# Reordering a second attention stage: earlier head loads, softmax and rotated queries at a higher priority, and another pace for weight sums

## The chip, the cores and the metric

The kernel runs on one core of a Trainium2 chip. The metric is the device time of one execution in microseconds (us). A core has five engines that run side by side: TensorE (PE; its weight loads are shown as PEld), VectorE (DVE), ScalarE (ACT), GpSimd (POOL) and SyncE (SP). SP does no arithmetic here; it issues the DMA transfers between DRAM and the on-chip memory, in its own order. POOL issues a second kind of DMA, one that can add to what stands in DRAM.

## The reference

Two decoder layers over 1024 tokens of width 1024, in float32. Layer 0 is a chunkwise mLSTM mixer and an MLP. From its output a shared key/value latent is computed once. Layer 1 is latent attention over it, and an MLP. What matters here is the attention of layer 1 (8 heads, 128 plain and 64 rotated columns per head) and the MLPs:

```python
def block(args):                       # one block of 128 queries, all heads
    s = (einsum('bqhd,bkhd->bhqk', qn_b, k_nope)
         + einsum('bqhd,bkd->bhqk', qr_b, k_rope)) * scale
    s = where(kpos[None, :] <= qpos[:, None], s, -inf)
    p = softmax(s, axis=-1)
    return einsum('bhqk,bkhd->bqhd', p, v)

def sqrelu_mlp(h, w1, w2):             # 1024 -> 4096 -> 1024
    return square(relu(h @ w1)) @ w2
...
x = x + g1 * rmsnorm(mixer(modulate(rmsnorm(x))))
x = x + g2 * rmsnorm(sqrelu_mlp(modulate(rmsnorm(x)), w1, w2))
```

## The kernel before

**Number format.** Every dense operand is kept as a high and a low part in float32r, and a product is three matmuls (`mm3`, lines 255 to 257: low by high, high by low, high by high). A weight block of 128x1024 is loaded by SP into a `raw` buffer (line 236; four buffers), cast to the high part `wh` by ACT (L549 or L190) and subtracted to the low part `wl` by DVE (L550 or L191). Activations are split in the same way (`split_mod`, L531 on ACT and L532 on DVE).

**Two halves, two streams.** The 1024 tokens go through as two halves of 512. While one half runs its mixer, the other runs an MLP whose products keep TensorE full: `two_streams(dense, other)` takes steps from the two generators in turn, and `go` ties every step's TensorE work behind the last one's, so that TensorE's order is the order written in the code. Three such stretches follow one another: the MLP of layer 0 for the first half; the MLP of layer 0 for the second half beside `attention_first`; the MLP of layer 1 for the first half beside `attention_second`. After them the last MLP runs alone; it uses sums of weight blocks and needs fewer products for that.

**The order on the other engines.** The order of each engine's instructions is fixed when the program is built. A planner simulates the engines on estimated durations and takes, of the instructions that are ready, the one of the highest priority; without more, that is the one traced first. `prompt(f)` raises the priority of what `f` traces by 300 places (`PRIO`). The dense stream's weight loads, its hidden activations and its accumulations (`accumulate`, L199) have this; the splits of its weights have 40 (`CUT`). On the chip every engine then follows its list in order.

**Attention.** `prepare_pair` computes for a pair of heads the keys, values, plain queries and rotated queries (`rope`, then `query_rotary`: a cast on ACT, L1565, and four pieces on DVE, L1567 to L1570). In the second half keys and values are stored to DRAM (`kd`, L1646; `vd`, L1652), and so are the queries (`qd`, L1668) and the rotated queries (`td`, L1669). After the four pairs, `units` in `attention_second` goes over the heads one by one: `loaded_head` reads a head back (two `kd` loads at L1681, `qd` at L1683, `td` of the pair at L1686, two `vd` loads at L1689; 512 KB each), and its two groups of 256 queries follow. All these tiles share 24 buffers of the tag `k4`.

For a group, `scores` computes two score tiles (`score_mm`, L1584 to L1590, into the PSUM tile `pm`, of which there are two, shared with the dense stream) and runs `softmax` on each: maximum (L1594), scaling of it (L1595), both on DVE, exponential with row sum on ACT (L1596), reciprocal (L1597) and multiplication (L1598) on DVE, and for the first of the two a zeroing of 128 columns on POOL (L1600). The probabilities stand in `raw` buffers. `turned` transposes them on TensorE (L1704) and splits the result with `split_mod`; `products` multiplies by the values one dense step later.

**Weight sums.** `weight_sums` prepares in DRAM, with POOL's adding DMAs, the four sums of blocks of `mlp_w1[1]` that the last MLP needs: 16 chunks of eight transfers of 256 KB, each a step of the generator `wsums`. A step is a DVE flag (L1046), tied behind the dense stream's latest DVE instruction, a POOL copy that waits for it (L1047) and the DMA (L1050 if it adds, else L1052). The dense streams take a step each time they finish one of their own: `with_weight_sums` for the first two stretches, once 28 steps have been counted, and `with_rest` for the third, one each until the 128 are used up.

Of the kernel before, what the change touches and what calls it, by code (L numbers as in the profile page):

```python
# [83 lines left out]
def kernel(  # L84
# [408 lines left out]
    def last_of(g):  # L493

        while True:
            try:
                next(g)
            except StopIteration as e:
                return e.value
# [1062 lines left out]
    def query_rotary(qr):  # L1562
        T = k4v(F32R)
        hi = tmp(F32R)
        nc.scalar.copy(hi, qr)  # L1565

        nc.vector.tensor_copy(T[0:64, 0], hi[0:64].bitcast(F32))  # L1567
        nc.vector.tensor_copy(T[64:128, 1], hi[64:128].bitcast(F32))
        nc.vector.tensor_sub(T[64:128, 0], qr[0:64], hi[0:64].bitcast(F32))
        nc.vector.tensor_sub(T[0:64, 1], qr[64:128], hi[64:128].bitcast(F32))  # L1570
        return T

# [19 lines left out]
    def softmax(f, pr, n, even):  # L1592
        m, l = small(1), small(1)
        nc.vector.reduce_max(m, f, axis=AX.X, negate=True)  # L1594
        nc.vector.tensor_scalar(m, m, SCALE, None, ALU.mult)  # L1595
        nc.scalar.activation(pr[:, :n], f, AF.Exp, bias=m, scale=SCALE, accum_out=l)  # L1596
        nc.vector.reciprocal(l, l)  # L1597
        nc.vector.tensor_scalar(pr[:, :n], pr[:, :n], l, None, ALU.mult)  # L1598
        if even:
            nc.gpsimd.memset(pr[:, n : n + P], 0.0)  # L1600

    def scores(kk, unit):

        (_, q, kn, _), j = unit
        prs = []
        if j < 2:
            st = pm()
            pr = raw().rearrange("p (a b) -> p a b", b=512)
            for e in range(2):
                score_mm(lambda g: st[:, e], kk, q, kn, 2 * j + e)  # L1610
            for e in range(2):
                n = (2 * j + e + 1) * P
                softmax(st[:, e, :n], pr[:, e], n, e == 0)
                prs.append(pr[:, e])
        else:
            for e in range(2):
                st = pm()
                n = (2 * j + e + 1) * P
                score_mm(lambda g: st[:, g], kk, q, kn, 2 * j + e)
                pr = raw()  # L1620
                softmax(st.rearrange("p a b -> p (a b)")[:, :n], pr, n, e == 0)
                prs.append(pr)
        return prs

# [6 lines left out]
    def prepare_pair(p_, hf):  # L1631


        wr, wkv = w_pair_r(p_), w_pair_kv(p_)
        yield 0
        wn, pt = w_pair_n(p_), pc()
        for k in range(3):
            mm3(pt, wr[0][:, k], wr[1][:, k], hf.cq[0][k], hf.cq[1][k], k == 0, k == 2)
        rp = rope(pt, hf)
        next(rp)  # L1640
        kt = [k4v(F32R) for _ in range(2)]
        kn = [(t[:, 0], t[:, 1]) for t in kt]
        k_half(kn, wkv, hf)
        for r in range(2):
            for i in range(2):
                nc.sync.dma_start(kd[2 * p_ + r, i, :, ts(hf.i, H)], kn[r][i].bitcast(F32))  # L1646
        yield 1
        vt = [k4v(F32R, 256) for _ in range(2)]
        v = v_half(wkv, hf, vt)
        for r in range(2):  # L1650
            for i in range(2):
                nc.sync.dma_start(  # L1652
                    vd[2 * p_ + r, i, :, ts(hf.i, H)].rearrange("p (t e) -> p t e", e=P),
                    vt[i][:, :, ts(r, P)].bitcast(F32),
                )
        qn = []
        for r in range(2):
            t = k4v(F32R)
            pt = pc() if r else ps()
            for k in range(3):  # L1660
                s = ts(r, P)
                mm3(pt, wn[0][:, k, s], wn[1][:, k, s], hf.cq[0][k], hf.cq[1][k], k == 0, k == 2)
            split_mod(t[:, 0], t[:, 1], pt, None)
            qn.append(t)
        T = query_rotary(last_of(rp))
        if hf.i:
            for r in range(2):
                nc.sync.dma_start(qd[2 * p_ + r], flat(qn[r]))  # L1668
            nc.sync.dma_start(td[p_], flat(T))  # L1669
            yield 1  # L1670
        else:
            yield 2
        vs = [[(h_[:, ts(r, P)], l_[:, ts(r, P)]) for h_, l_ in v] for r in range(2)]
        return [(2 * p_ + r, (qn[r], T[:, r]), kn[r], vs[r]) for r in range(2)]
# [18 lines left out]
    def attend(hf, groups, dense, behind=lambda: None):  # L1693


        def turned(work):
            PTh, PTl = hdv(F32R, 256), hdv(F32R, 256)
            n = 0
            for u, b0, nb in work:
                for b in range(b0, b0 + nb, 2):  # L1700
                    pt = pc()
                    for e in range(2):
                        for i in range(2):
                            nc.tensor.transpose(  # L1704
                                pt[:, ts(2 * e + i, P)], u.prs[i][:, ts(b + e, P)], ident
                            )
                    s = slice(n, n + 2)
                    split_mod(PTh[:, s], PTl[:, s], pt.rearrange("p (a b) -> p a b", b=256), None)
                    n += 2
            return PTh, PTl  # L1710

        def products(work, PT):
            n = 0
            for u, b0, nb in work:
                if b0 == 0:
                    u.po = ps()[:, :256]
                for kb in range(b0, b0 + nb):
                    mm3(u.po, *u.v[kb], PT[0][:, n], PT[1][:, n], kb == 0, kb == u.nk - 1)
                    n += 1
                if b0 + nb == u.nk:  # L1720
                    s = ts(u.j % 2, 256)
                    if u.hh < 6:
                        o = tmp()[:, :256]
                        nc.scalar.copy(o, u.po)
                        nc.sync.dma_start(oT[ts(u.hh, P), ts(u.j, 256)], o)
                    else:
                        split_mod(hf.o.hi[u.hh][:, s], hf.o.lo[u.hh][:, s], u.po, None)

        def begin():
            us = []  # L1730
            for head, j in next(groups, []):
                u = Half()
                (u.hh, _, _, u.v), u.j, u.nk = head, j, 2 * j + 2
                u.prs = scores(hf.kk, (head, j))
                us.append(u)
            return us

        late = None
        yield "align"
        us = begin()  # L1740
        yield 1
        while us:
            if sum(u.nk for u in us) <= 4:
                rounds = [[(u, 0, u.nk) for u in us]]
            else:
                rounds = [[(u, b, min(4, u.nk - b))] for u in us for b in range(0, u.nk, 4)]
            for n, work in enumerate(rounds):
                if late:
                    late()
                PT = turned(work)  # L1750
                late = lambda a=(work, PT): products(*a)
                if len(rounds) == 1:
                    yield 1
                if n == len(rounds) - 1:
                    us = begin()
                    if not us:
                        behind()
                yield next(dense)
        late()
# [15 lines left out]
    def attention_second(hf):  # L1775
        pairs = [prepare_pair(p_, hf) for p_ in range(4)]
        next(pairs[0])
        yield 0
        for p_ in range(4):
            if p_ < 3:  # L1780
                yield from primed(pairs[p_], pairs[p_ + 1])
            else:
                yield from pairs[p_]

        def units():
            for hh in range(NH):
                h_ = loaded_head(hh)
                if hh == 6:
                    last_o(hf)
                for j in range(2, 4):  # L1790
                    yield [(h_, j)]

        yield from attend(hf, units(), cycle((1, 0.5, 0.5)), lambda: load_o(hf))
# [364 lines left out]
    wsums = weight_sums(mlp_w1[1])  # L2158
    steps_done = [0]

    def with_weight_sums(g):
        for v in g:
            if v != "within":
                steps_done[0] += 1
                if steps_done[0] > 28:
                    next(wsums, None)
            yield v

# [76 lines left out]
    def with_rest(g):  # L2245

        n = 0
        for v in g:
            if v != "within":
                n += 1  # L2250
                next(wsums, None)
                if n == 61:
                    later[0]()
            yield v
# [18 lines left out]
    n = 0  # L2273
# [34 lines left out]
```

## Time and profile before

| what | us |
|---|---|
| median of three runs | 2362.25 (2359.37 to 2362.75) |
| the profiled execution | 2359.22 |
| its span, first to last instruction | 2357.3 |
| TensorE busy | 2321.8 |
| VectorE busy | 1605.7 |
| ScalarE busy | 1098.2 |
| GpSimd busy | 155.0 |

The span is what the trace covers; the time is what the device reports and is 1.9 us longer. "Busy" is the time in which an engine has an instruction in work. TensorE's instructions overlap, so a busy TensorE may still start its matmuls further apart than it could; the distance between two starts tells that. A row of the timeline has the start, the duration, the engine and line, the operation, the tile written and the tiles read, and in brackets how long the engine had been idle and what released it. "SPq" and "POOLq" are the queues' own entries.

### The profile page before, as it was taken

The page shows a single profiled execution, that of the slowest core. Times are in us where ns is not written, and L with a number is a line of the kernel's source. Part 1 is how long each engine was busy: PE and PEld are TensorE (multiplying, and loading weights), DVE is VectorE, ACT ScalarE, POOL GpSimd, SP SyncE. Part 2 cuts the span into 40 slices and gives each one's busy share as a digit, 9 for nine tenths or more (in the row PEclk, how much of TensorE's full clock was granted, in tenths as well). Part 3 has the DMA queues.
Part 4 walks back from the last instruction along what each step waited for, and adds up shares of the span by engine and source line. Part 5 has one row for each costly group of instructions (what it writes and reads, how often), then busy time and mean ns, then how long its engine had stood idle before and what let it go on. Part 6 is the DMA issues. An engine that isn't in the chain of part 4 may idle for free.

```text
span 2357.3 us, 32527 instructions
## 1 busy us (share of the span) xinstructions
PE 2321.8 (98%) x12181; PEld 1959.9 (83%) x12181; DVE 1605.7 (68%) x2657; ACT 1098.2 (47%) x1826; POOL 155.0 (7%) x353
## 2 busy tenths in 40 slices
PE   7999999999999999999999999999999999999998
PEld 5888898888888888888888888888888888989997
DVE  6677876867685777777764967765656488557556
ACT  4355335654343354334444554434444445655543
POOL 1010000000001110111010110010001000000000
PEclk9999999999999999999999999999999999999999
DMA  9452664545566876667764665885544553656562
GB/s 314 144 153 82 191 184 149 156 141 163 174 184 179 284 222 188 184 195 207 211 160 126 199 200 183 274 274 172 163 134 134 143 164 97 185 173 217 166 185 88
DMA packets 408349, 420.76 MB, mean 178 GB/s; under 512 B 27427, under 2 KB 310112, under 8 KB 404608
## 3 DMA queue, kind: packets, MB, share of 16 engines
q1 hardware_dynamic: 402272, 385.02, 52.1%
q0 software_dynamic: 5920, 33.66, 6.5%
q8 instruction: 96, 1.57, 0.3%
q14 instruction: 61, 0.50, 0.1%
HBM read 359.37 MB, written 92.80 MB: 192 GB/s over the span
## 4 chain that ended last, share of the span: by engine, by line
PE 89%; DVE 5%; DMA 4%; ACT 1%; issue 1%; SPq 0%; DVEq 0%; ACTq 0%
PE ps L255 15%; PE ps L257 15%; PE ps L256 15%; PE pm L255 10%; PE pm L256 10%; PE pm L257 10%; DMA raw<-in_mlp_w_dram 2%; PE pc L256 2%; PE pc L257 2%; PE pc L255 2%; PE pc L1704 1%; DMA raw<-in_a_w_in_dram 1%; PE pm L1590 1%; PE pm L899 1%; PE pm L1584 1%
## 5 line engine op out<-in xcount | busy, mean ns | idle before, releaser
L255 PE MATMUL ps<-k,wl 128*128 128x512 f32 (+1 forms) x1432 | 546.3, 381 | 1.6 <-DVE wl L191 1.3
L257 PE MATMUL ps<-k,wh 128*128 128x512 f32 (+1 forms) x1432 | 539.0, 376 | 0.0
L256 PE MATMUL ps<-k,wh 128*128 128x512 f32 (+1 forms) x1432 | 537.4, 375 | 0.0
L549 ACT CAST wh<-raw 128x1024 fp32r<-128x1024 f32 x272 | 285.0, 1051 | 481.4 <-PE ps L255 149.0
L550 DVE TENSOR_TENSOR wl<-raw,wh 128x1024 fp32r<-128x1024 f32 x272 | 331.7, 1221 | 249.4 <-ACT wh L549 155.4
L255 PEld LDWEIGHTS ps<-k,wl 128*128 128x128 f32 x1432 | 269.6, 188 | 53.7 <-issue 3.6
L257 PEld LDWEIGHTS ps<-k,wh 128*128 128x128 f32 x1432 | 269.4, 188 | 50.1 <-issue 0.7
L256 PEld LDWEIGHTS ps<-k,wh 128*128 128x128 f32 x1432 | 269.8, 188 | 48.9 <-issue 1.7
L199 DVE TENSOR_TENSOR k<-k,pm 128x512 f32<-128x512 f32 (+1 forms) x254 | 210.9, 858 | 83.3 <-PE pm L257 82.0
L191 DVE TENSOR_TENSOR wl<-raw,wh 128x1024 fp32r<-128x1024 f32 (+2 forms) x110 | 128.1, 1166 | 115.6 <-ACT wh L190 115.4
L255 PE MATMUL pm<-hd,wl 128*128 128x512 f32 x512 | 201.4, 393 | 0.5 <-ACT hd L531 0.5
L256 PE MATMUL pm<-hd,wh 128*128 128x512 f32 x512 | 199.3, 390 | 0.2 <-DVE hd L532 0.2
L257 PE MATMUL pm<-hd,wh 128*128 128x512 f32 x512 | 199.3, 390 | 0.0
L255 PE MATMUL pm<-wh,hd 128*128 128x512 f32 x488 | 192.2, 394 | 2.9 <-ACT raw L1596 2.5
L256 PE MATMUL pm<-wl,hd 128*128 128x512 f32 x488 | 190.3, 390 | 0.0
L257 PE MATMUL pm<-wh,hd 128*128 128x512 f32 x488 | 190.2, 390 | 0.0
L190 ACT CAST wh<-raw 128x1024 fp32r<-128x1024 f32 (+2 forms) x110 | 109.4, 996 | 172.3 <-PE ps L255 82.9
L1596 ACT ACTIVATE raw<-pm,sm 128x128 f32<-128x128 f32 (+3 forms) x64 | 47.5, 742 | 152.4 <-DVE sm L1595 122.8
L532 DVE TENSOR_TENSOR hd<-tmp,hd 128x512 fp32r<-128x512 f32 x128 | 88.0, 688 | 38.6 <-ACT hd L531 37.9
L255 PEld LDWEIGHTS pm<-hd,wl 128*128 128x128 f32 x512 | 96.2, 188 | 21.0 <-ACT hd L531 0.9
L256 PEld LDWEIGHTS pm<-hd,wh 128*128 128x128 f32 x512 | 96.2, 188 | 20.5 <-DVE hd L532 0.5
L257 PEld LDWEIGHTS pm<-hd,wh 128*128 128x128 f32 x512 | 96.1, 188 | 20.1
(391 smaller groups left out, 4274.9 us busy)
## 6 DMA issues: line engine op xcount, KB each, us to landing
raw<-in_mlp_w_dram SPq DMA_DIRECT2D x240, 512.0 KB, 4.3
raw<-in_ada_w_dram SPq DMA_DIRECT2D x80, 512.0 KB, 4.6
raw<-in_a_w_in_dram SPq DMA_DIRECT2D x48, 512.0 KB, 4.4
sums<-in_mlp_w_dram POOLq DMA_DIRECT2D x96, 256.0 KB, 4.5
raw<-sums SPq DMA_DIRECT2D x64, 256.0 KB, 3.7
xs<-k SPq DMA_DIRECT2D x40, 256.0 KB, 5.6
raw<-in_kv_ada_w_dram SPq DMA_DIRECT2D x16, 512.0 KB, 4.1
raw<-in_a_w_out_dram SPq DMA_DIRECT2D x16, 512.0 KB, 4.9
```

The source lines that it names most:

```text
L190: nc.scalar.copy(hi[:, :n], r[:, :n])
L191: i = nc.vector.tensor_sub(lo[:, :n], r[:, :n], hi[:, :n].bitcast(F32))
L199: return f(*a, **k)
L255: nc.tensor.matmul(o, ll, rh, start=start, stop=False, **m)
L256: nc.tensor.matmul(o, lh, rl, start=False, stop=False, **m)
L257: pe_last[0] = nc.tensor.matmul(o, lh, rh, start=False, stop=stop, **m)
L532: nc.vector.tensor_sub(lo, u, hi.bitcast(F32))
L549: nc.scalar.copy(hi, u)
L550: nc.vector.tensor_sub(lo, u, hi.bitcast(F32))
L899: nc.tensor.matmul(nv[:, r, i], hf.PT[p_][:, r, cs], v[2 * p_ + r], start=g == 0, stop=True,)
L1584: nc.tensor.matmul(o[:, :w], ql, kh, start=True, stop=False)
L1596: nc.scalar.activation(pr[:, :n], f, AF.Exp, bias=m, scale=SCALE, accum_out=l)
```

## The change

Five things are changed.

- `softmax` is traced with `prompt`, in both branches of `scores`, so in both attention stages.
- `query_rotary` is traced with `prompt`, in every pair of both halves. `rope`, which feeds it, is not.
- The `split_mod` of the turned probabilities is traced with `prompt`.
- In the second half, `loaded_head(0)` is called inside `prepare_pair` of the last pair, ahead of that pair's `qd` and `td` stores; `units` uses the head that was loaded there.
- `with_weight_sums` starts after 44 counted steps in place of 28. `with_rest` takes one sum a step for steps 1 to 11, none for steps 12 to 22, and two a step from step 23 on.

```diff
@@ scores
-                softmax(st[:, e, :n], pr[:, e], n, e == 0)
+                prompt(softmax)(st[:, e, :n], pr[:, e], n, e == 0)
...
-                softmax(st.rearrange("p a b -> p (a b)")[:, :n], pr, n, e == 0)
+                prompt(softmax)(st.rearrange("p a b -> p (a b)")[:, :n], pr, n, e == 0)
@@ prepare_pair
-        T = query_rotary(last_of(rp))
+        T = prompt(query_rotary)(last_of(rp))
         if hf.i:
+            if p_ == 3:
+                hf.first = loaded_head(0)
             for r in range(2):
                 nc.sync.dma_start(qd[2 * p_ + r], flat(qn[r]))
             nc.sync.dma_start(td[p_], flat(T))
@@ turned
-                    split_mod(PTh[:, s], PTl[:, s], pt.rearrange("p (a b) -> p a b", b=256), None)
+                    prompt(split_mod)(
+                        PTh[:, s], PTl[:, s], pt.rearrange("p (a b) -> p a b", b=256), None
+                    )
@@ units
-                h_ = loaded_head(hh)
+                h_ = loaded_head(hh) if hh else hf.first
@@ with_weight_sums
-                if steps_done[0] > 28:
+                if steps_done[0] > 44:
                     next(wsums, None)
@@ with_rest
-                next(wsums, None)
+                for _ in range(1 if n < 12 else 0 if n < 23 else 2):
+                    next(wsums, None)
```

## The prediction

> **What bounds the kernel now.** I read the busy line first, then a table by stage, then what TensorE waited for in the two attention stages, and last the timeline around the longest of those waits.
>
> ```profile
> PE 2321.8 (98%) x12181; PEld 1959.9 (83%) x12181; DVE 1605.7 (68%) x2657; ACT 1098.2 (47%) x1826; POOL 155.0 (7%) x353
> ```
>
> The span is 2357.3 us, so TensorE (PE) is without work for 35.5 us in all. No reordering of the other engines can win more than what PE idles where they touch it. The stage table says where that is.
>
> ```profile
> core 0: us, PE busy (x) PEld busy (x) DVE busy (x) ACT busy (x) POOL busy (x), PEclk, DMA share, GB/s
> 960.00:1200.00 240.00, 235.91 (x1230) 198.06 (x1229) 182.82 (x349) 99.33 (x188) 29.28 (x69) 1.00 0.66 188
> 1200.00:1560.00 360.00, 359.32 (x1641) 297.49 (x1640) 248.01 (x374) 173.69 (x264) 42.37 (x91) 1.00 0.66 200
> 1560.00:1860.00 300.00, 295.18 (x1617) 250.85 (x1616) 179.20 (x314) 127.19 (x214) 25.24 (x65) 1.00 0.55 169
> 1860.00:2340.00 480.00, 479.98 (x2773) 423.61 (x2772) 299.15 (x431) 249.92 (x415) 0.00 (x0) 1.00 0.52 157
> ```
>
> First attention (960 to 1200) idles 4.1 us, the stretch to the last pair's queries 0.7, second attention (1560 to 1860) 4.8. The rest of the 35.5 lies at the two ends of the program, which the diff does not touch. So even a perfect change wins about 4.1 + 0.7 + 4.8 = 9.6 us. The clock is 1.00 throughout and plays no part. Below are PE's waits, three rows of 1560 to 1860 and two of 940 to 1240 (total, times, longest).
>
> ```profile
> PE pm L255 <- ACT raw L1596: 2.5, 4, 1.1
> PE pm L1586 <- DMA k<-td: 1.1, 1, 1.1
> PE pc L1704 <- DVE raw L1598: 0.5, 3, 0.2
> ...
> PE pm L1584 <- DVE k L199: 2.9, 4, 0.9
> PE pm L1584 <- DVE sm L1046: 1.2, 3, 0.5
> ```
>
> In second attention two things are late: once the rotated queries of the first head, read back from DRAM (td), and four times the exponential that frees a score tile (pm) for the dense product. In first attention it is the dense accumulation (L199) that frees pm late for the scores.
>
> **The change part by part.** *First head's loads ahead of the last pair's stores.* The timeline, SyncE's queue (SPq) with the engines it waits for:
>
> ```profile
> 1555.33 3.45 SPq L1668 DMA_DIRECT2D qd<-k  x2
> 1557.74 0.69 DVE L532 TENSOR_TENSOR k<-pc,k 128x512 fp32r<-128x512 f32 x1
> 1558.83 1.26 SPq L1681 DMA_DIRECT2D k<-kd  x2
> 1560.71 0.38 SPq L1686 DMA_DIRECT2D k<-td  x1
> 1561.28 0.69 DVE L1570 TENSOR_TENSOR k<-tmc,tmp 64x512 fp32r<-64x512 f32 x1
> 1561.99 0.32 SPq L1669 DMA_DIRECT2D td<-k  x1
> 1566.90 0.39 PE L1585 MATMUL pm<-k,k 128*128 128x512 f32 x1
> 1568.39 0.50 PE L1586 MATMUL pm<-hd,k 128*128 128x512 f32 x1 [1.10 <-DMA k<-td]
> ...
> k<-td SPq DMA_DIRECT2D x4, 512.0 KB, 6.9
> ```
>
> The two qd stores sit at the head of SPq for 3.45 us, because the second needs the query split that ends at 1558.43. The loads stand behind them, td at 1560.71, and it lands 7.6 us later, when the score product starts at 1568.39. Loads traced first no longer stand behind the stores, so td is issued some 3.4 us sooner, at about 1557.3, and by the same 7.6 us lands at 1564.9. PE wants it 0.23 after 1566.90, at 1567.13, so 2.2 us are left over. Worth: 1568.39 - 1567.13 = **-1.3**. Bounds: -1.3, and 0 if the loads still wait, for a buffer for instance. The stores are moved too: two qd and one td, three issues. The data of qd are ready at 1558.43, those of td at 1561.97 (L1570). Between today's first store entry and first load SPq spends 3.5 us waiting, and the loads up to td take 1.9 (1558.83 to 1560.71), so the loads fit into the waiting, and the stores go out at most some 1 us later than today. Only the reloads of the last two heads, late in the stage, read them, and the buffers that they free are for later heads: 0, and without that cover the 1 us. Late next after td are the head's values (vd), used only after a dense step, and PE shows no wait for them: 0.
>
> *Softmax ahead.* The worst of the four waits, with what stands ahead of the softmax:
>
> ```profile
> 1591.20 8.58 DMA raw<-in_mlp_w_dram
> ...
> 1600.88 1.23 DVE L550 TENSOR_TENSOR wl<-raw,wh 128x1024 fp32r<-128x1024 f32 x1 [4.30 <-ACT wh L549]
> 1602.03 0.82 DVE L1594 TENSOR_REDUCE sm<-pm 128x1 f32<-128x640 f32 x1
> 1602.76 0.68 DVE L532 TENSOR_TENSOR hd<-tmp,hd 128x512 fp32r<-128x512 f32 x1
> 1603.36 0.15 DVE L1595 TENSOR_SCALAR sm<-sm 128x1 f32<-128x1 f32 x1
> 1603.37 0.36 PE L1590 MATMUL pm<-k,k 128*128 128x256 f32 x1
> 1604.52 0.17 DVE L1597 RECIPROCAL sm<-sm 128x1 f32<-128x1 f32 x1 [1.01 <-ACT raw L1596]
> 1604.54 0.50 PE L255 MATMUL pm<-wh,hd 128*128 128x512 f32 x1 [0.81 <-ACT raw L1596]
> 1605.19 1.28 DVE L532 TENSOR_TENSOR hd<-pc,hd 128x512 fp32r<-128x512 f32 x2
> 1606.39 0.95 DVE L1594 TENSOR_REDUCE sm<-pm 128x1 f32<-128x768 f32 x1
> 1607.17 0.39 PE L257 MATMUL pm<-wh,hd 128*128 128x512 f32 x1
> 1608.68 0.50 PE L255 MATMUL pm<-wh,hd 128*128 128x512 f32 x1 [1.13 <-ACT raw L1596]
> ```
>
> Start to start PE loses 1.17 - 0.12 = 1.05 at 1604.54 and 1.51 - 0.23 = 1.28 at 1608.68, 2.3 together. VectorE (DVE) works in order: it idled 4.30 us behind a weight split (L550) whose load took 8.58 us, and the maximum of the scores stood behind that split. Priority decides between instructions that are ready together when the order is planned; a weight split planned as ready before the scores stays ahead, and so does the older split of the turned probabilities (L532 x2), which gets the same priority. What can still move is the single L532 of 0.68 between maximum and scaling. I take **-0.7**, that one instruction once. Bounds: -3.0, the 2.5 and 0.5 of PE's own waits, and the other way +4.8, four accumulations L199 (four waits above), each put behind one more maximum of at most 1.2 us (L1594 took 0.82 and 0.95 here for 640 and 768 columns; 1024 by the same slope 1.2). I stay near the small end, since the rows show DVE held by a late transfer, not by a choice between ready instructions.
>
> [...]
>
> *Rotated queries and turned probabilities ahead.* The rotary's last DVE piece ends at 1561.97 and PE needs none of it there (the attention reads head 0 from DRAM); the turned probabilities are read only after a dense step. 0 both; without that cover one split of 0.68 each.
>
> *Weight sums.* 128 sums as before, each a DVE flag, a POOL copy and a POOL DMA of 256 KB.
>
> ```profile
> L1046 DVE MEMSET sm<- x128: 59/59/59, 695.5 to 1822.6; 128x1 f32 x128
> ...
> 1570.00:1580.00 10.00, 10.00 (x53) 8.37 (x52) 4.00 (x10) 4.36 (x9) 0.97 (x2) 1.00 1.03 390
> 1592.63 0.52 POOL L1052 DMA_DIRECT2D sums<-sums  x1
> ...
> 1608.90 0.06 DVE L1046 MEMSET sm<- 128x1 f32 x1
> ```
>
> By the code 24, 64 and 40 sums fall into the three dense stretches; afterwards 8, 64 and 56, because the first begins 16 steps later. The 40th of the last stretch is the flag at 1822.6; counting flags back, the 22nd is the one at 1608.90. So the pause (steps 12 to 22) covers about 1509 to 1609, and the rate doubles after it, until step 45. In the pause the weight load issued at 1591.20 no longer shares the engines with the sum of 1592.63: 256 KB at the 390 GB/s of that neighbourhood are 0.66 us, and the chain L550, L1594, L1596 moves by it: **-0.7** (bounds 0 and -2.3, the whole pair of stalls). After the pause 23 extra sums, one more per step, each able to delay a load by the same 0.66; PE shows it only where a head's loads stand ahead of the weights, of which one comparable place is left beyond the pair above: I take **+0.4** (bounds 0 and 4 x 0.66 = +2.6, one for each pm wait). The sixteen sums gone from the first stretch: PE has no gap there, 0.
>
> Sum: -1.3 - 0.7 - 0.7 + 0.4 = **-2.3 us**. The profiled execution took 2359.22 us for a span of 2357.3; it would become 2356.9. Its time is 3.0 below the median of the runs, 2362.25, which becomes 2359.95, say **2360.0**. 0.2% is 4.7 us, about what a measurement of this kernel can tell from no change, so this is no change.
>
> **The rivals.** *Priorities do reorder DVE (faster).* If the maximum of the scores is planned ahead of L550 and L532, the four pm waits go (-2.5 visible, 2.3 of it start to start at one place alone), and less competition frees pm in first attention too (a quarter of 4.1, -1.0): with td and the sums -1.3 - 2.5 - 1.0 - 0.7 = -5.5, 2356.8. For it: DVE idled 1.01 us before 1604.52 while the second tile's scores were nearly done (L1590 at 1603.37), and their maximum came only at 1606.39. Against: both orders are planned on durations in which the weights need not be late.
>
> *The weights fall behind six loads (slower).* The loads now come in one run ahead of weight loads on the same queue.
>
> ```profile
> DMA to landing us min/median/max: 3.3/5.0/12.8
> ```
>
> That is L236, the weights, from 1560 to 1860: 5.0 typical, 8.58 where three head loads stood ahead, and that lateness of 3.6 cost 2.3 at PE. Six loads are 3 MB, 8.1 us at 390 GB/s; against the 3.6 this is 4.5 more, and since DVE takes its work in order, the last pair's evacuations (L532) wait behind the split: 2.3 + 4.5 = 6.8, less td's 1.3, +5.5, 2367.8. It decides once a weight split is planned ahead of those evacuations. Against: SPq is blocked there today, so nothing that now goes out sooner is a weight load that comes later.
> [...]
>
> *Two sums a step hold POOL (slower).* The zeroing that the transposes need (L1600) shares POOL with the sums.
>
> ```profile
> 1366.53 0.76 POOL L1050 DMA_DIRECT2D sums<-in_mlp_w_dram  x1 [6.54 <-DMA sums<-sums]
> ...
> 1588.54 0.20 POOL L1600 MEMSET raw<- 128x128 f32 x1 [3.33 <-DVE wl L550]
> ...
> 1593.54 1.38 PE L1704 MATMUL pc<-ident,raw 128*128 128x128 f32 x8
> ```
>
> A sum that needs the one before it waits 6.54 us for it to land. By the order of the eight sums of a chunk this happens inside a pair once in four steps, five times in 23. A zeroing behind it has 5.0 us to spare (1588.54 to 1593.54): 1.5 us each, 5 x 1.5 = +7.5, less 1.3 and 0.7, +5.5, 2367.8. It decides where the landing takes more than 5 us. Against: the zeroing, part of softmax, gets priority.
>
> *The loads do not move* (no free buffer): 0 - 0.7 - 0.7 + 0.4 = -1.0, 2361.3, no change.
>
> **How the numbers follow.** Forecast as summed 0.39, loads not moved 0.05, reordered DVE 0.36, weights late 0.11, POOL held 0.09. So faster 0.36, same 0.44, slower 0.20. Range 2353.5 to 2366.5: below, the faster case and most of the 9.6 us of idle in reach; above, most of the slower cases short of their full price. The likeliest case alone, by the bounds of its terms kept inside 0.2%: 2357.6 to 2366.
>
> **What would show it.** Td: in the profile after, the k<-td load of head 0 issued before the last pair's qd stores, and no wait of L1586 on td. Softmax: L1595 right behind L1594, and fewer or shorter waits of L255 on L1596; if the four remain, the reordering did nothing. Sums: no L1046 between about 1509 and 1609, then pairs; L236 landing later than 5.0 in the median, or L1600 behind a wait on sums, speaks for the slower cases. The prediction is wrong if PE's idle time in 960 to 1860 falls or grows by more than 4.7 us, or if a stage that now shows none gains some.

## The result, and the profile after

The changed kernel took 2381.13 us (median of six runs, 2378.08 to 2382.23), the kernel before on the same chip 2362.5 (six runs, 2358.35 to 2364.51). The ratio is 1.008 with a 95% interval of 1.0067 to 1.0093: 18.6 us slower, where no change was forecast. The profiled execution took 2381.32 us, 22.1 more than that of before, which had come out 3 us below its own median.

From the page of the changed kernel, the busy line:

```profile
span 2379.6 us, 32559 instructions
## 1 busy us (share of the span) xinstructions
PE 2328.9 (98%) x12181; PEld 1965.0 (83%) x12181; DVE 1607.8 (68%) x2657; ACT 1097.7 (46%) x1826; POOL 154.9 (7%) x353
```

The number of instructions on every engine is that of before. The work is the same; only its order and its gaps differ. The stage table of the changed kernel, in the columns of the prediction's table (stretch, length, busy time of PE, PEld, DVE, ACT, POOL, granted clock, DMA share, GB/s):

```profile
360.00:960.00 600.00, 589.37 (x2645) 483.96 (x2644) 415.56 (x611) 282.64 (x410) 20.81 (x52) 0.99 0.56 173
960.00:1200.00 240.00, 235.09 (x1216) 197.02 (x1215) 186.47 (x342) 98.67 (x181) 27.30 (x66) 1.00 0.68 196
...
1560.00:1860.00 300.00, 292.16 (x1609) 248.91 (x1608) 183.76 (x340) 126.04 (x214) 41.76 (x97) 0.99 0.60 181
```

The first row is the one to look at. In the same stretch of the kernel before PE had no gap at all:

```profile
360.00:960.00 600.00, 600.00 (x2707) 493.48 (x2707) 427.70 (x648) 287.89 (x416) 37.03 (x87) 1.00 0.62 187
```

So 10.6 us of idle time appeared in the first dense stretch, where the change only takes away sixteen weight sums. The waits of PE in the changed kernel (total, times, longest) name the two places, and a third in second attention:

```profile
PE ps L255 <- DVE wl L550: 6.3, 1, 6.3
PE pm L255 <- ACT raw L1596: 5.4, 5, 3.8
PE pm L255 <- DVE wl L550: 4.3, 1, 4.3
...
PE pm L1586 <- DMA k<-td: 0.5, 1, 0.5
```

For a full account I took the start times of all matmuls of both traces and compared, number by number, by how much the same matmul starts later in the changed kernel. In all it is 22.3 us, the difference of the spans: 1.9 up to the first long wait (in that part the profiles of the kernels below lie between 1.1 us ahead of the kernel before and 3.2 behind it), **14.8 in the first dense stretch** from there on, 1.5 in first attention (where the other profiles are between 1.6 shorter and 2.8 longer), **4.2 in second attention**, nothing elsewhere.

**The first dense stretch.** DVE of the kernel before, with the flags of two sums (L1046) and the preparation of latent weights (L1403 to L1408), which is background work. The timeline has start, duration, engine and line, operation, tiles:

```profile
742.61 0.07 DVE L1046 MEMSET sm<- 128x1 f32 x2
...
747.69 0.28 DVE L1414 TENSOR_REDUCE lbias<-pc 128x1 f32<-128x128 f32 x1
747.89 0.28 DVE L1403 TENSOR_SCALAR tma<-raw,kvada 128x128 f32<-128x128 f32 x1
...
750.91 1.22 DVE L1408 TENSOR_TENSOR raw<-raw,mods 128x1024 f32<-128x1024 f32 x1
```

And the same work in the changed kernel, DVE and ACT, up to the matmul that waits (rows of other engines left out):

```profile
749.60 0.28 DVE L1414 TENSOR_REDUCE lbias<-pc 128x1 f32<-128x128 f32 x1
...
755.99 0.69 DVE L532 TENSOR_TENSOR hd<-tmp,hd 128x512 fp32r<-128x512 f32 x1 [6.11 <-ACT hd L531]
...
756.60 0.28 DVE L1403 TENSOR_SCALAR tma<-raw,kvada 128x128 f32<-128x128 f32 x1
...
761.00 1.22 DVE L1408 TENSOR_TENSOR raw<-raw,mods 128x1024 f32<-128x1024 f32 x1
762.26 1.04 ACT L190 CAST wh<-raw 128x1024 fp32r<-128x1024 f32 x1 [6.30 <-DVE raw L1408]
763.21 2.93 ACT L549 CAST wh<-raw 128x1024 fp32r<-128x1024 f32 x3
...
763.33 1.23 DVE L191 TENSOR_TENSOR wl<-raw,wh 128x1024 fp32r<-128x1024 f32 x1 [1.11 <-ACT wh L190]
764.48 3.49 DVE L550 TENSOR_TENSOR wl<-raw,wh 128x1024 fp32r<-128x1024 f32 x3
...
765.75 0.80 PE L255 MATMUL ps<-k,wl 128*128 128x512 f32 x1 [6.30 <-DVE wl L550]
```

Before, the latent work begins 0.2 us after L1414. After, it lets 7 us pass (749.60 to 756.60) in which DVE idles for 6.11, until the dense step's own last DVE instruction (L532) has run. The casts that wait for it are first in ACT's list (L190), and the casts of the dense weights (L549), two of whose loads went out from 739.96 on and had landed by 748, stand behind them. PE runs dry for 6.3 us, and 23 us later once more for 4.3.

The reason lies in the code, in a line that the prediction did not look at. Background work is traced under `paced()`, tied behind `pace[0]`, and `two_streams` sets that after every dense step (line 2113 of the kernel before):

```python
pace[0] = next(i for i in reversed(traced) if i.engine == dve)
```

This is the DVE instruction traced last. While sums are issued, it is the flag of a sum, which is itself only tied behind the pace before it, which is a flag again: for the background work the tie is all but void. Without the sums it is the dense step's last real instruction, so the background work comes one dense step later, and with it everything that stands behind it on ACT.

**Second attention.** The chain that ends in the 3.8 us, from the changed kernel's timeline (waits in brackets; rows of other work left out):

```profile
1703.87 1.44 SPq L1683 DMA_DIRECT2D k<-kd  x2
...
1705.40 0.38 SPq L1685 DMA_DIRECT2D k<-qd  x1
1705.84 0.42 SPq L1691 DMA_DIRECT2D k<-vd  x1
...
1706.36 0.38 SPq L236 DMA_DIRECT2D raw<-in_mlp_w_dram  x1
...
1707.32 1.22 POOL L1050 DMA_DIRECT2D sums<-in_mlp_w_dram  x1 [0.27 <-issue]
...
1708.45 0.71 POOL L1052 DMA_DIRECT2D sums<-in_mlp_w_dram  x1
...
1717.34 1.05 ACT L549 CAST wh<-raw 128x1024 fp32r<-128x1024 f32 x1 [4.51 <-DMA raw<-in_mlp_w_dram]
...
1718.42 1.23 DVE L550 TENSOR_TENSOR wl<-raw,wh 128x1024 fp32r<-128x1024 f32 x1 [7.34 <-ACT wh L549]
...
1719.56 0.82 DVE L1594 TENSOR_REDUCE sm<-pm 128x1 f32<-128x640 f32 x1
1720.29 0.68 DVE L532 TENSOR_TENSOR hd<-tmp,hd 128x512 fp32r<-128x512 f32 x1
1720.89 0.15 DVE L1595 TENSOR_SCALAR sm<-sm 128x1 f32<-128x1 f32 x1
...
1721.13 0.79 ACT L1596 ACTIVATE raw<-pm,sm 128x640 f32<-128x640 f32 x1 [0.60 <-DVE sm L1595]
```

It is the chain of the prediction at another head (the sixth; the prediction's was the third): four head loads ahead of a weight load, the split behind it, the softmax behind the split. With both sums of a doubled step beside it the weight takes 11.0 us from issue (1706.36) to the cast (1717.34). In the kernel before, the chain of waits has the same weight, behind the same four head loads and with one sum beside it (start, length):

```profile
1688.06 8.05 DMA raw<-in_mlp_w_dram
```

There PE waits 0.4 us for the softmax, here 3.8.

**The loads.** SP's queue in the changed kernel, around the last pair's stores:

```profile
1573.49 3.46 SPq L1670 DMA_DIRECT2D qd<-k  x2
1576.99 1.27 SPq L1683 DMA_DIRECT2D k<-kd  x2
...
1578.89 0.38 SPq L1688 DMA_DIRECT2D k<-td  x1
```

The stores are still at the head for 3.46 us, with the loads behind them: traced earlier, planned in the same order.

### The profile page after: what moved, and what is told of

It is laid out like the page before. It is cut to its first block, busy times and chain, and to the rows that moved or that the text cites. A ratio compares the mean times of both kernels' runs of the same rounds, so it can differ in the third digit from the quotient of the medians.

```text
span 2379.6 us, 32559 instructions
## 1 busy us (share of the span) xinstructions
PE 2328.9 (98%) x12181; PEld 1965.0 (83%) x12181; DVE 1607.8 (68%) x2657; ACT 1097.7 (46%) x1826; POOL 154.9 (7%) x353
## 4 chain that ended last, share of the span: by engine, by line
PE 88%; DVE 5%; DMA 4%; ACT 1%; issue 1%; SPq 0%; DVEq 0%; ACTq 0%
PE ps L255 15%; PE ps L256 15%; PE ps L257 15%; PE pm L255 10%; PE pm L256 10%; PE pm L257 10%; DMA raw<-in_mlp_w_dram 2%; PE pc L256 2%; PE pc L255 2%; PE pc L257 2%; PE pc L1706 1%; DMA raw<-in_a_w_in_dram 1%; PE pm L1590 1%; DVE tma L383 1%; PE pm L899 1%
## 5 line engine op out<-in xcount | busy, mean ns | idle before, releaser
L549 ACT CAST wh<-raw 128x1024 fp32r<-128x1024 f32 x272 | 284.7, 1050 | 483.8 <-PE ps L255 143.6
L550 DVE TENSOR_TENSOR wl<-raw,wh 128x1024 fp32r<-128x1024 f32 x272 | 332.1, 1223 | 254.9 <-ACT wh L549 164.6
L190 ACT CAST wh<-raw 128x1024 fp32r<-128x1024 f32 (+2 forms) x110 | 109.4, 996 | 177.8 <-PE ps L255 81.7
L532 DVE TENSOR_TENSOR hd<-tmp,hd 128x512 fp32r<-128x512 f32 x128 | 88.2, 690 | 50.1 <-ACT hd L531 49.5
```

The lines of the kernel that those rows point to most:

```text
L190: nc.scalar.copy(hi[:, :n], r[:, :n])
L532: nc.vector.tensor_sub(lo, u, hi.bitcast(F32))
L549: nc.scalar.copy(hi, u)
L550: nc.vector.tensor_sub(lo, u, hi.bitcast(F32))
```

## The experiments

Four theories stood beside each other. *Pace*: the loss in the first stretch comes from what `pace[0]` points to. *Transfers*: it comes from the moved 256 KB transfers themselves. *Weights late*: the loss in second attention comes from sums beside weight loads that stand behind head loads on one queue. *Priorities*: DVE's new order costs time.

**Which part loses the time.** The changed kernel with only the start put back (`44` to `28`), and the kernel before with only that changed (`28` to `44`):

> The changed kernel with one number put back: the sums of the first stretch start after 28 steps again, not 44. Theory (pace): the 16 flags (L1046) that no longer stand in the first stretch were what the background work was tied to; without them the latent weights' DVE work (L1403 to L1408, L191) is tied to the dense step's own last DVE instruction, one step later, holds the load buffers longer, and PE waits for two weight splits (6.3 and 4.3 us). With 28 back both waits are gone: about 14.7 us less, some 2366.5 us, 1.002 of before. Rival A (doubled sums of the last stretch are the cost): nearly all of the 18.6 us stays, 2379 or more. Rival B (the priorities are the cost): the same, 2379.

> The kernel before with one number changed: the sums of the first stretch start after 44 steps. Theory (pace): the same two waits of PE on L550 in the first stretch, between 740 and 800, 6 and 4 us, and about 14.7 us more than before, some 2377 us. Rivals A and B: no loss, 2362 us.

The first took 2364.55 us, 1.0018 (1.0008 to 1.0028) of the kernel before (2362.08 in this group); the second 2376.32, 1.0066 (1.005 to 1.0082). The waits of the second:

```profile
PE ps L255 <- DVE wl L550: 6.3, 1, 6.3
PE pm L255 <- DVE wl L550: 4.3, 1, 4.3
```

They are those of the changed kernel to the tenth, and the first kernel has neither. One number in the code is worth 14.2 us alone (2376.32 - 2362.08). Within the change it is 0.0062 by the ratios (1.008 - 1.0018), some 14.6 us; the medians themselves, 2381.13 and 2364.55, are of two groups of runs.

**Pace or transfers.** To tell these apart, the changed kernel got only flags for the steps 29 to 44, with no copy and no transfer, and the kernel before kept its transfers from step 28 on, while the pace skipped their flags up to step 44:

```diff
# flags kept, in the changed kernel
                 if steps_done[0] > 44:
                     next(wsums, None)
+                elif steps_done[0] > 28:
+                    with paced():
+                        nc.vector.memset(small(1), 0.0)
# pace from the dense step, in the kernel before
-                pace[0] = next(i for i in reversed(traced) if i.engine == dve)
+                pace[0] = next(
+                    i for i in reversed(traced)
+                    if i.engine == dve and not (steps_done[0] <= 44 and id(i) in flags)
+                )
```

> The changed kernel (start after 44), but at each of the steps 29 to 44 of the first stretch a bare DVE flag of 60 ns is set in the same way, with no POOL copy and no DMA behind it. Theory (pace): what is missing in the first stretch is only the flag that loosens the pace, so PE's two waits on L550 there go and the time is as with the start after 28, some 2366 us. Rival C (it is the sums' DMAs or POOL work that are missing there or come at a bad time later): as the changed kernel, 2381 us.

> The kernel before with its sums where they are (start after 28, all DMAs), but for the steps up to 44 the instruction that background work is tied behind is the dense step's own last DVE instruction, and never a flag. Theory (pace): the two waits of PE on L550 appear although every sum is issued as before: about 14.7 us more, 2377 us. Rival C (the sums' absence): no loss, 2362 us.

Sixteen memsets of 0.06 us win the time back: 2364.52 us, 1.0012 (1.0002 to 1.0021). And the kernel before, with every transfer where it was, loses it: 2377.02, 1.0066 (1.0047 to 1.0084). Its waits (an inserted line shifts the numbers by one, so L551 is L550):

```profile
PE ps L256 <- DVE wl L551: 6.3, 1, 6.3
PE pm L256 <- DVE sm L1047: 4.3, 1, 4.3
```

In this kernel a flag sits behind the last split, which is why it is named in the second row. That settles the first stretch: the pace, not the transfers.

**The priorities and the loads.** The three `prompt` calls and the loads traced ahead, with both paces of the sums as before:

> The three priorities and the earlier trace of the first head's loads alone; both paces of the sums as before. Theory (order stays): the priorities hardly change any engine's order and the loads stay behind the stores on SPq, so the time is that of before within 0.1%, td's wait of 1.1 us and the four waits on the exponential (2.5) remain. Rival D (priorities free pm sooner, as the prediction's faster case had it): 2 to 5 us less.

2359.95 us against 2361.09 in this group, 0.9996 (0.9987 to 1.0004). No measurable effect, as expected here; the -2.0 us that the prediction summed for these parts lies within the interval too. The trace has the waits that were to stay: 3.2 us for the exponential, four times, and 0.6 for td.

**The pace of the last stretch.** First the whole of it in the kernel before (one, none, two sums a step), then its two halves apart: the pause alone (`1 if n < 12 else 0 if n < 23 else 1`), and the doubling alone (one up to step 22, then two):

> The kernel before with the pace of the sums in the last stretch alone: one a step, none for steps 12 to 22, then two. Theory (doubled sums): the weight load behind a head's three or four loads lands at 10 to 11 us in place of 8, VectorE's split of it stands ahead of the softmax, and one wait of PE on the exponential grows to 3 to 4 us: second attention loses about 4 us more, 2365 to 2366. Rival E (the pause, or the pace of the background work, is what costs): the same loss, but with PE waits elsewhere than behind a late weight load. Rival F (that wait is chance): as before, 2362.

> The kernel before with the pause alone: no sums in steps 12 to 22 of the last stretch, one a step before and after. Theory (doubled sums): the rate is never doubled, so no wait of PE on the exponential above 2 us, second attention as before, 2361 to 2363. Rival E (the pause, which takes flags from the pace of eleven steps): the loss of the whole pace edit, about 4 us, 2365.

> The kernel before with the doubling alone: one sum a step up to step 22, two from step 23 until the 128 are used up. Theory (doubled sums): two sums now stand beside the weight load that follows the head loads near 1690, it lands at 10 us or more, and PE waits 3 to 4 us there for the exponential; some 3 us more, 2364 to 2365. Rival E (pause): as before, 2362.

The whole: 2365.82 us, 1.0019 (1.001 to 1.0028). The pause: 2359.44, 0.9991 (0.9983 to 1.0; before 2360.51). The doubling: 2364.52, 1.0014 (1.0005 to 1.0023). So the doubling costs some 3.3 us (0.0014 x 2360.5; 1.2 to 5.4 by the interval) and the pause nothing. Doubling alone, the first of PE's waits in second attention:

```profile
PE pm L255 <- ACT raw L1596: 6.7, 5, 4.2
```

And from the same kernel's chain of waits the weight load ahead of the longest of them (start, length):

```profile
1686.94 11.99 DMA raw<-in_mlp_w_dram
```

Two sums were issued within 0.64 us of each other 1.4 us behind that load, and it took 12 us; the wait behind it is 4.2. By the starts of the matmuls second attention is longer than before by 3.6 to 6.3 us in the five profiles that have the doubled sums beside head loads on SP's queue, and by -0.4 to 2.0 in the five that have single sums there.

The number of sums is not all that the new pace changes. Beside this load the kernel before has one sum that overwrites (L1052), the changed kernel has one of these and one that adds (L1050), the doubling alone two that add. In eleven profiles the load took 8.0 to 9.6 us in the first case, 10.1 to 11.0 in the second, 12.0 in the third. And in the pause alone, a single sum that adds comes to stand beside the weights of two other heads, for one of them here:

```profile
1621.77 0.79 POOL L1050 DMA_DIRECT2D sums<-in_mlp_w_dram  x1 [0.28 <-issue]
```

These two weights took 9.5 and 9.3 us. In the other kernels they took 7.7 to 8.6 and 7.3 to 8.6 beside a single overwriting sum, 9.2 to 10.2 and 9.3 to 9.9 beside one of each. At those two places the kind of the sum makes the difference, and the second sum hardly adds to it. At the place of the long wait no run has a single adding sum, so there the kind and the number are not told apart.

**The loads in the promised order.** Here the kernel before got the loads ahead, and the last pair's stores tied behind the td load:

```diff
-            for r in range(2):
-                nc.sync.dma_start(qd[2 * p_ + r], flat(qn[r]))
-            nc.sync.dma_start(td[p_], flat(T))
+            with tc.issue_after(hf.td_load) if p_ == 3 else nullcontext():
+                for r in range(2):
+                    nc.sync.dma_start(qd[2 * p_ + r], flat(qn[r]))
+                nc.sync.dma_start(td[p_], flat(T))
```

> The kernel before with the first head's loads traced ahead of the last pair's stores, and these stores tied behind the td load, so that the order on SPq really changes. Theory (the prediction's first step, with the order enforced): td is issued about 3 us sooner, its wait of 1.1 us goes, 1.3 us less, some 2361, all else as before. Rival G (the loads wait for buffers and hold SPq, with the weights behind them): td no sooner and a new wait of PE on a weight split, 2 us or more lost.

Its queue shows the order, and its waits in second attention (all of them above 0.2 us) no td:

```profile
1560.56 0.32 SPq L1692 DMA_DIRECT2D k<-td  x1
...
1562.21 1.41 SPq L1672 DMA_DIRECT2D qd<-k  x2
```

```profile
PE pm L255 <- ACT raw L1596: 4.7, 4, 2.1
```

The wait for td (1.1) is gone, as the prediction reckoned for it, but that for the late softmax is 4.7 in place of 2.5. The profiled execution was the longest of the eleven, though (2364.14 us), and the time, a median of 2359.59, 0.9992 (0.9983 to 1.0001), can't be told from no change.

**The weights off the head loads' queue.** If head loads ahead of weight loads are the cause, the head loads on another queue must free the weights. All loads in `loaded_head` go from `nc.sync` to `nc.gpsimd`; then only the keys and values; then all of them together with the new pace of the last stretch:

> The kernel before with the loads of all eight heads issued by GpSimd and not by SP, so that a weight load no longer stands behind them in one queue. Theory (late weights behind head loads make the waits on the exponential): the weight loads of 1560 to 1860 land at 4 to 6 us with none at 8 or above next to a head's loads, and the waits of PE L255 on L1596, 2.5 us, largely go: 2 to 4 us less. Rival H (the transfers share the same engines anyway, or the loads now wait on POOL behind the sums): the waits stay or td comes later, 0 to 5 us more.

> The kernel before with only the keys and values of the heads (four of the loads, 2 MB) issued by GpSimd; the plain and rotated queries stay on SyncE. Theory (queue order): at most two head loads still stand ahead of a weight load, the waits on the exponential nearly go (under 0.8 us in all), and the queries no longer wait behind POOL's other work, so the 0.8 us wait on qd of the kernel with all head loads on GpSimd goes too: 2357 to 2359, at least as good as that one. Rival H (shared engines): waits near 2.5 us and 2361.

> All head loads on GpSimd and the changed pace of the last stretch (pause, then two sums a step). Theory (doubled sums hurt only a weight load that stands behind head loads on SyncE's queue): no wait on the exponential above 1 us, so within 1 us of the kernel with the loads on GpSimd alone, about 2358. Rival I (two sums a step slow every load, or hold GpSimd): the loss of about 4 us comes back, 2362 or more.

All moved, waits of PE in second attention:

```profile
PE pm L1584 <- DVE k L199: 0.9, 1, 0.9
PE pm L1584 <- DMA k<-qd: 0.8, 1, 0.8
...
PE pm L255 <- ACT raw L1596: 0.2, 1, 0.2
```

The late softmax is gone but for 0.2 us. SP's queue shows why. In the kernel before, the head loads wait in it for the buffers that the scores of an earlier head free, and the weights wait behind them; with all head loads on POOL, the weight that went out at 1688.06 goes out at 1679.28, ahead of its head's loads (1684.00), and lands after 4.9 us. The first row is a wait of SP's queue before, the second an entry of it with the loads on POOL:

```profile
SPq L1681 <- PE pm L1585: 43.6, 5, 10.5
...
1679.28 0.37 SPq L236 DMA_DIRECT2D raw<-in_mlp_w_dram  x1
```

The time is 2358.29 us against 2361.09, 0.9985 (0.9976 to 0.9994): the only version here with an interval below one, ahead of both kernels, by less than the 0.2% that the prediction counted as no change. With the doubled pace on top, 2360.03, 0.9993 (0.9984 to 1.0002; before 2360.51), and that wait stays at 0.5: the doubling no longer finds weights to delay there. But PE waits longer for the last head's query load, 2.0 us in place of 0.8 (in an execution of 2364.92 us, the longest of the twelve):

```profile
PE pm L1584 <- DMA k<-qd: 2.0, 1, 2.0
```

Against the version without the doubling the two ratios differ by 0.0008 and their intervals overlap, so a rest of its cost is neither shown nor excluded.

The half measure missed its expectation: 2366.03 us, 1.0021 (1.0012 to 1.0029). Left on SP's queue, the first query load is planned behind the stores, and the scores wait for it:

```profile
PE pm L1584 <- DMA k<-qd: 4.3, 1, 4.3
PE pm L255 <- ACT raw L1596: 4.1, 4, 1.5
```

The second row is a miss too: it was to fall below 0.8. With the queries left on SP's queue a weight still goes out behind a query load, at 1693.02, while keys and values go out on POOL's at 1691.98 to 1693.05, and it took 9.6 us. Fewer head loads ahead of it in its own queue were not enough; what the full move brought is that the weights go out before the head loads.

The median landing of a weight in second attention hardly moved: 4.8 us with the head loads on POOL, 5.0 before. What changed is which transfer stands behind which, and with it when the weights go out.

## Why the prediction was wrong

**The step that failed** is "The sixteen sums gone from the first stretch: PE has no gap there, 0." It asked what the removed work had cost, found no gap that its going could close, and stopped. It did not ask what else was tied to that work. The flags were the instructions that `pace[0]` pointed to. Their going costs 14.8 us by the starts of the matmuls, shown from both sides: kept without transfers, the loss goes; skipped with transfers in place, it comes. No term and no rival covers it, and so 2353.5 to 2366.5 missed by 14.6. The prediction did name its sign: wrong "if a stage that now shows none gains some". Its other sign did not come: PE's idle time in 960 to 1860 went from 9.6 to 13.4 us, by less than 4.7.

**The clock** "plays no part" held for before, not for after. The two waits are 10.6 us, the loss there is 14.8: see the last section.

**Weight sums in the last stretch.** The mechanism was right, the size not. The doubling was taken at +0.4, with +2.6 as the bound; it measured +3.3 alone (1.2 to 5.4), and second attention of the changed kernel lost 4.2. The prediction assumed that a sum delays a load by its own bytes at full rate, 0.66 us, whatever its kind. The load beside two adding sums took 12.0 us, against 8.05 at the same place before with one overwriting sum: 3.9 more. Not every load was slowed: the median landing of a weight in second attention is 5.1 us in the changed kernel, 5.0 before. The pause, at -0.7, did what it was to do at its place. The weight of the third head, 8.6 us before, took 7.8 in the kernel with the pause alone, and the first wait of the prediction's pair is at most 0.4 us in the five profiles with the pause, 0.8 to 1.4 in the six without it; the second, 0.8 to 1.1, stayed. A wait of 1.3 at the sixth head makes up for it there, so that the sum is 2.6 as before 2.5, and the time, 0.9991 (0.9983 to 1.0), leaves -0.7 open.

**The loads ahead.** The term of -1.3 assumed that what is traced first is planned first. The rival "the loads do not move", with a chance of 0.05, held. Forced into that order, the load removes the wait as reckoned. In that one profile PE then waits longer for the softmax behind the weights, while "late next after td" was named as the values; the time shows neither a gain nor a loss.

**Priorities.** The terms for the rotated queries and turned probabilities, 0, stood; for the softmax, -0.7 did not take place. L532 still runs between L1594 and L1595 (1720.29 above). That fits the reason given for staying near the small end, an order planned on durations in which no weight is late; no run tests the reason. So the likeliest rival, "Priorities do reorder DVE", with a chance of 0.36, is not borne out: with the priorities and loads alone the four waits remain (3.2 us).

**The rivals.** "Weights fall behind six loads" named the right neighbourhood but another cause: not the loads moved but the sums beside them. "Two sums a step hold POOL" isn't borne out: in second attention of the changed kernel PE waits for the softmax and for td, and never for POOL's zeroing (L1600). That the pm waits stay (3.2 us, four times, with the priorities and loads alone) is not for want of pm tiles: with the head loads on POOL they all but go, from 2.5 us before to 0.2, with two of these tiles as before. The changed kernel with the old start is left at 1.0018, which is what the last stretch's pace alone gives (1.0019): with that the change is accounted for in the runs. Why the plan keeps the loads behind the stores stays open, as do the 1.5 us in first attention, which other profiles differ by as well.

## What to carry to other kernels

Before an instruction is taken away, however small, look up who holds a reference to it: an anchor found as "the last one traced" changes its meaning with whatever is traced there. A stage without a gap has nothing to win, but all to lose, so price what the removal lets happen, not only what it saves. And when a transfer is late, look first at what stands ahead of it in its own queue and what that waits for; moving all of those loads to another queue, so that the late ones went out earlier, all but removed a wait here that the new priorities had left in place (2.5 us before, 3.2 with the priorities, 0.2 with the loads moved), and moving only a part of them made it worse (4.1).

## What the runs showed of the hardware

The long waits cost more than their length. The changed kernel, just after the wait of 6.3 us and from 770 us on (columns as in the stage table; the clock is the third from last):

```profile
766.00:768.00 2.00, 2.00 (x5) 1.59 (x6) 1.96 (x2) 0.14 (x1) 0.00 (x0) 0.50 1.02 231
...
770.00:780.00 10.00, 10.00 (x46) 8.23 (x45) 2.24 (x4) 1.85 (x3) 0.00 (x0) 1.00 0.55 145
```

At the granted clock of 0.50 matmuls start 0.43 us apart, not 0.23, for 8 of them here, about 10 after the wait of 4.3, 6 after that of 3.8 in second attention, 14 after that of 4.2 in the kernel with the doubling alone. At 0.2 us each the 8 and the 10 add 3.6 to the two waits of 10.6 us, which makes 14.2 of the 14.8 measured. The kernel before has no such stretch between its ends: its granted clock is 1.00 from 33.2 to 2350.8 us.

The slow starts lasted 3.4 us after the wait of 6.3 (8 x 0.43), 4.3 after that of 4.3, 2.6 after that of 3.8, and 6.0 after that of 4.2. Shorter gaps were followed by them too: with the loads forced first, two starts 2.44 us apart by eight slow ones, and in the changed kernel two starts 1.55 us apart at 267 us by eight as well, at a granted clock of 0.50 from 267.50 to 270.91. These eight make up 1.5 of the 1.9 us lost up to the first long wait. At the same place of the kernel before, two starts 1.54 us apart were followed by none, at a clock of 1.00. So the length of the gap alone does not decide it here, and what else does no run shows.
